# A two-block network with 64 routed experts on one core: another cut of the first expert blocks, token rows kept once in fp32, 18 weight buffers, another end

## The chip, the core and the metric

The kernel runs on one core of a Trainium2 chip, in one launch. The core has TensorE (PE, whose weight loads the profile lists as PEld), VectorE (DVE), ScalarE (ACT), GpSimd (POOL) and SyncE (SP), which here issues nearly all loads. The metric is the device time of one launch in microseconds; the profile has a span, from the first to the last instruction, and the time of its own execution, which is a little longer.

## What is computed

512 tokens of 1024 numbers pass an even and an odd attention layer, then a Fourier and state-space mixer, and at last 64 routed experts and a norm. All but the last two stay as they are, so only these are shown.

```python
hn = _rmsnorm(x, ffn_norm_g[i])
x = x + _hier_moe(hn, ...)          # and then _rmsnorm(x, final_norm_g)

def _hier_moe(h, wg, bg, we, be, w_gate, w_up, w_down):
    g_prob = softmax(ht @ wg + bg);  p_g, g_idx = top_k(g_prob, 1)      # one of 8 groups
    e_sel = (ht @ we + be) of that group                                # its 8 experts
    top_l, top_i = top_k(e_sel, 2)
    gate_w = p_g * softmax(top_l);  expert = g_idx * 8 + top_i
    ...
    def expert_block(args):                                             # per expert, on its tokens
        a = jax.nn.silu(xb @ w_gate[e]) * (xb @ w_up[e])
        return a @ w_down[e]
    ...
    y = y_pad[dest] * w_s[:, None]
    out = segment_sum(y, tok_s, num_segments=t)                         # two experts per token, added
```

All is fp32. An expert has three weights of 2 MB (`w_gate`, `w_up` 1024x512, `w_down` 512x1024), 384 MB in all, each read once.

## The kernel before

The residual stream is kept transposed as `h[k]`, eight tiles of 128 features by 512 tokens. `mix` ends with eight steps; behind each of them `feed3(k)` takes the new `h[k]`: its squares for the norm, its scaled copy for the router's matmul (`self.logits`, 72 rows), and its transposes into token rows, four 128x128 blocks on PE. The rows are written three times: unscaled into `x3`, the running sum of the residual and the experts; and times the norm's gain as a high and a low fp32r part `hn`.

`route` is a chain of small DVE operations with some matmuls: logits, best group, best two experts, the place of each token within its expert (`slot`), the rank of the experts by count, a table of tokens and weights per block (`tab`). The work is cut into blocks of 128 rows. The first four experts are fixed, so their blocks need no ranking; the others are sorted by count, and the fullest come next. The first eight (`WIDE`) experts stand two to a block with 64 rows each, the 56 others four to a block with 32 rows each: 18 blocks. What doesn't fit is done by `moe_rest`, a loop that runs as often as there are experts with more tokens than rows (no pass in the profiled execution: each of the three weights is issued x128, which is what the blocks need).

Per pair of blocks `slot_rows` makes 0/1 selection matrices on DVE, and `rows` gathers the tokens' rows transposed by matmuls with them (L1979, hi and lo part one after the other). Per block `hidden` does the gate and up matmuls (L1997), `turned` four transposes, `result` the down matmuls (L2020); `combine` adds the rows back into `x3` by matmuls (L1942, L1943) and DVE additions (L1944). The experts of a block stand side by side on PE, each on its own columns. `moe_pairs` orders this: it puts parts of the previous block's combine and the next pair's gather into the present block.

The weights come as tiles `ew` of 128x2048 fp32 (1 MB), two per weight, 384 in all, on SP's queue in the order of use (`moe_pieces`, `moe_prefetch`). A tile takes the next buffer of a rotation (`w_tile`): four opened while the mixer still runs (`m_e0`, `E_EARLY`) and eleven after it (`m_e`, `E_MORE`). A load waits on SP until the last matmul that reads its buffer is done, and all later loads wait behind it. The last two blocks are ordered apart: their gate and up tiles first, then the down tiles, the very last of them fetched by columns (`by_col`), so that the results can be finished half by half (`last_results`, L1955 to L1963) with the final norm right behind them (`final`, L2080 to L2094).

## Time and profile before

| | before |
|---|---|
| median of 3 runs | 2388.55 us (2381.56 to 2389.39) |
| profiled execution | 2389.68 us |
| its span | 2387.9 us |
| mean granted TensorE clock | 0.958 of full speed |
| busy in the span: PE, DVE, ACT, POOL | 89%, 47%, 28%, 18% |
| DMA over the span | 546.35 MB, mean 229 GB/s |

The strip of the page cuts the span into 40 equal slices and gives busy tenths for each engine, the granted clock, and GB/s. The chain that ended last is followed back from the last instruction. In timelines a row is one instruction or a few like it, with its start; the idle time before it and what ended that stand in brackets.

### The profile page before, as it was taken

The numbers are of one execution on the slowest core, as the hardware profiler recorded it, in microseconds if no ns is written. First come the engines' busy times: TensorE is split into PE (matmuls) and PEld (weight loads), VectorE is DVE, ScalarE is ACT, GpSimd is POOL, SyncE is SP. The second block draws the span as 40 slices with busy tenths as digits, with TensorE's granted clock in tenths as the row PEclk, the third lists the DMA queues.
The fourth block names the chain that finished last, engine by engine and source line by source line (L and its number), as shares of the span: only waits on it lengthen the run. The fifth ranks groups of instructions, "written<-read, shape, count | busy, mean of one in ns | idle before, by whom it ended". The sixth has DMA issues, their size and how long they took to land. (4 is left out here: it accounts for less than half of the span.)

```text
span 2387.9 us, 30369 instructions
## 1 busy us (share of the span) xinstructions
PE 2132.0 (89%) x11370; PEld 1398.3 (59%) x11370; DVE 1116.5 (47%) x2239; ACT 665.3 (28%) x1278; POOL 437.7 (18%) x473
## 2 busy tenths in 40 slices
PE   8989998999999999999999969988888888787865
PEld 7878886887788888889868744432222222222311
DVE  7687869674455665665744542421111111111102
ACT  6623223335445555543325410000000000000001
POOL 1235655300024333311311400000000000000000
PEclk9989999999999999989999979999999999999988
DMA  5213334554221212124352477999999999999996
GB/s 187 86 59 108 113 105 138 146 167 161 76 89 45 71 54 63 54 67 151 108 167 87 170 294 318 383 400 420 421 421 421 421 421 421 421 421 421 420 421 237
DMA packets 110832, 546.35 MB, mean 229 GB/s; under 512 B 13552, under 2 KB 14493, under 8 KB 62554
## 3 DMA queue, kind: packets, MB, share of 16 engines
q1 hardware_dynamic: 105834, 529.66, 58.0%
q0 software_dynamic: 4528, 13.67, 1.7%
q8 instruction: 91, 1.49, 0.3%
q10 hardware_dynamic: 320, 1.05, 0.1%
...
HBM read 531.22 MB, written 15.20 MB: 229 GB/s over the span
## 5 line engine op out<-in xcount | busy, mean ns | idle before, releaser
L1997 PE MATMUL mps<-ew,xt 128*32 128x512 f32 (+1 forms) x2048 | 391.1, 654 | 89.1 <-DMA ew<-in_w_up 48.8
L314 PE MATMUL ps<-uh,wh 128*128 128x512 f32 (+1 forms) x728 | 291.9, 401 | 7.7 <-ACT uh L309 7.3
L316 PE MATMUL ps<-uh,wl 128*128 128x512 f32 (+1 forms) x728 | 287.6, 395 | 3.5 <-DVE wl L345 3.5
L343 ACT ACTIVATE wh<-wraw 128x1024 fp32r<-128x1024 f32 (+5 forms) x187 | 186.8, 999 | 368.8 <-PE ps L315 268.7
L315 PE MATMUL ps<-ul,wh 128*128 128x512 f32 (+1 forms) x728 | 287.0, 394 | 0.5 <-DVE ul L310 0.5
L1997 PEld LDWEIGHTS mps<-ew,xt 128*32 128x32 f32 (+1 forms) x2048 | 93.2, 121 | 330.2 <-issue 164.3
L2020 PE MATMUL mps<-ew,s 128*32 128x512 f32 (+1 forms) x960 | 226.2, 620 | 38.5 <-DMA ew<-in_w_down 28.3
L345 DVE TENSOR_TENSOR wl<-wraw,wh 128x1024 fp32r<-128x1024 f32 (+4 forms) x172 | 218.4, 1270 | 49.1 <-ACT wh L343 47.2
L2082 POOL TENSOR_TENSOR ew<-x,ew 128x512 f32<-128x512 f32 x4 | 5.0, 1281 | 933.9 <-DVE x L1963 933.9
L2020 PEld LDWEIGHTS mps<-ew,s 128*32 128x32 f32 (+1 forms) x960 | 57.1, 115 | 195.4 <-issue 100.5
L314 PEld LDWEIGHTS ps<-uh,wh 128*128 128x128 f32 (+1 forms) x728 | 138.0, 190 | 39.9 <-ACT uh L309 7.3
L316 PEld LDWEIGHTS ps<-uh,wl 128*128 128x128 f32 (+1 forms) x728 | 137.6, 189 | 34.5 <-DVE wl L345 4.1
L315 PEld LDWEIGHTS ps<-ul,wh 128*128 128x128 f32 (+1 forms) x728 | 137.8, 189 | 28.4 <-DVE ul L310 1.0
L310 DVE SCALAR_TENSOR_TENSOR s<-mps,tab,s 128x512 fp32r<-128x512 f32 x36 | 27.0, 750 | 260.8 <-ACT s L309 260.0
L309 ACT ACTIVATE s<-mps,tab 128x512 fp32r<-128x512 f32 x36 | 24.8, 688 | 421.3 <-PE mps L2020 407.0
L2002 DVE SCALAR_TENSOR_TENSOR s<-mps,tab,s 128x512 f32<-128x512 f32 x18 | 13.5, 751 | 268.6 <-PE mps L1997 267.0
L314 PE MATMUL ps<-yh,wh 128*128 128x512 f32 x320 | 130.2, 409 | 1.9 <-DVE s L310 1.9
L316 PE MATMUL ps<-yh,wl 128*128 128x512 f32 x320 | 128.0, 400 | 1.7 <-DVE wl L345 1.7
L315 PE MATMUL ps<-yl,wh 128*128 128x512 f32 x320 | 128.9, 403 | 0.4 <-DVE yl L300 0.2
L1007 POOL TENSOR_SCALAR s<-s,n_sm 128x128 f32<-128x128 f32 (+3 forms) x96 | 110.1, 1165 | 8.4 <-DVE n_sm L998 4.9
L1944 DVE TENSOR_TENSOR x<-mps,x 128x512 f32<-128x512 f32 x128 | 83.6, 686 | 47.0 <-PE mps L1943 46.9
L2001 ACT ACTIVATE s<-mps,tab 128x512 f32<-128x512 f32 x18 | 12.4, 688 | 313.9 <-PE mps L1997 313.9
...
## 6 DMA issues: line engine op xcount, KB each, us to landing
ew<-in_w_gate SPq DMA_DIRECT2D x128, 1024.0 KB, 19.8
ew<-in_w_up SPq DMA_DIRECT2D x128, 1024.0 KB, 19.8
ew<-in_w_down SPq DMA_DIRECT2D x128, 1024.0 KB, 19.8
...
b<-in_od_w SPq DMA_DIRECT2D x32, 256.0 KB, 4.5
...
```

What stands on the lines that cost most here:

```text
L309: self.nc.scalar.activation(hi, src, AF.Copy, scale=col)
L310: self.nc.vector.scalar_tensor_tensor(lo, src, col, hi, ALU.mult, ALU.subtract)
L314: mm(out, l[0], r[0], start=start, stop=False)
L315: mm(out, l[0], r[1], start=False, stop=False)
L316: mm(out, l[1], r[0], start=False, stop=stop)
L343: nc.scalar.activation(hi, raw, AF.Copy)
L345: (nc.gpsimd if on_pool else nc.vector).tensor_tensor(lo, raw, hi, ALU.subtract)
L1007: nc.gpsimd.tensor_scalar(p[:, :w_], p[:, :w_], sm[:, br, hh:hh + 1], None, ALU.mult)
L1944: nc.vector.tensor_tensor(self.x3[:, b, cs], o, self.x3[:, b, cs], ALU.add)
L1997: nc.tensor.matmul(o[rs], xt[k][:, c0 + z * m:c0 + z * m + m], self.expert_rhs(w[i][z], k, 512, 0, 512), start=k == 0, stop=k == KD - 1)
L2002: nc.vector.scalar_tensor_tensor(act, h[1], r, act, ALU.mult, ALU.mult)
L2020: self.nc.tensor.matmul(y[hf][rs], at[:, k, rs], self.expert_rhs(w[-1][r], k, D, hf * 512, 512), start=k == 0, stop=k == 3)
```

## The change

`FIXED, WIDE` become 4, 4: block 0 has the four fixed experts with 32 rows each (24 tiles), blocks 1 and 2 have the four fullest ranked ones with 64 rows each (12 tiles), 14 blocks of four follow: 17 blocks. Block 0 has a gather of its own, 128 rows wide; blocks 1 and 2 share the next one, which now stands ahead of block 0's transposes. Eight weight buffers are opened early and ten later, 18 in all.

The rows are kept once, in fp32 and without the gain (`hn`). The gain is a 128x8 tile (`gperm`) and is applied when the gathered rows leave PSUM. The gather is one fp32 matmul where two fp32r ones were. `x3` is first written by block 0's combine. The transposes of `h[4]` to `h[7]` move from `feed3` into `route`, with their copies on ScalarE. At the end the previous block is combined before `last_results`, which then adds only its own rows, and the final norm takes one reciprocal root for all four token blocks. Small tiles move between pools.

```diff
-FIXED, WIDE = 4, 8
-BLOCKS = WIDE // 2 + (64 - WIDE) // 4
-GROUPS = BLOCKS // 2
+FIXED, WIDE = 4, 4
+BLOCKS = 1 + WIDE // 2 + (64 - FIXED - WIDE) // 4
+GROUPS = 1 + BLOCKS // 2
 SH_RET = 2
 NSA_FILL = 1, 2, 2, 2
-E_EARLY, E_MORE = 4, 11
+LATE = 4
+E_EARLY, E_MORE = 8, 10
...
-        self.hn = [self.t(self.mp, [P, NB, KD, P], "hn" + x, F32R) for x in "hl"]
+        self.hn = self.t(self.mp, [P, NB, KD, P], "hn")
...
-        tp = self.ps("tr")
-        self.transposes(tp, [(b * P, h[:, b * P:(b + 1) * P]) for b in range(NB)])
-        tv = tp.rearrange("p (b d) -> p b d", b=NB)
-
-        xg, g = self.s([P, NB, P]), self.gr[k // 4][:, k % 4 * P:k % 4 * P + P]
-        nc.vector.tensor_tensor(xg, tv, g.unsqueeze(1).to_broadcast([P, NB, P]), ALU.mult)
-        nc.vector.tensor_copy(self.x3[:, :, k * P:(k + 1) * P], tv)
-        hi, lo = (y[:, :, :, 16 * k:16 * k + 16] for y in self.hn)
-        xg = xg.rearrange("p b (m k) -> p b k m", k=KD)
-        nc.scalar.activation(hi, xg, AF.Copy)
-        nc.gpsimd.tensor_tensor(lo, xg, hi, ALU.subtract)
+        if k < LATE:
+            self.into_rows(k, nc.vector.tensor_copy)
         for j in range(max(0, k - 1), k if k < KD - 1 else KD):
             nc.tensor.matmul(self.logits[:72], self.wr[j // 4][:, j % 4], self.gx[j], start=j == 0, stop=j == KD - 1)
-        if k % 2 == 0 and len(self.early) < E_EARLY:
+        if len(self.early) < E_EARLY:
             self.moe_prefetch(len(self.early) + 1)
+
+    def into_rows(self, k, copy):
+
+        tp = self.ps("tr")
+        self.transposes(tp, [(b * P, self.h[k][:, b * P:(b + 1) * P]) for b in range(NB)])
+        copy(self.hn[:, :, :, 16 * k:16 * k + 16], tp.rearrange("p (b m k) -> p b k m", b=NB, k=KD))
...
-        self.gr = [self.load(self.bcast(a["ffn_g"], 512, c), [P, 512], y(x)) for c, x in ((0, "yh"), (512, "yl"))]
+        self.gperm = self.load(bass.AP(tensor=a["ffn_g"].tensor, offset=a["ffn_g"].offset, ap=[[KD, P], [1, KD]]), [P, KD],
+                               lambda sh: self.t(self.mp, sh, "gperm"))
...
+        for k in range(LATE, KD):
+            self.into_rows(k, nc.scalar.copy)
...
+        def further(out, pos):
+
+            v.tensor_scalar(out, pos, float(FIXED), 32.0, ALU.is_ge, ALU.mult)
+            v.scalar_tensor_tensor(out, pos, float(FIXED + WIDE), out, ALU.is_lt, ALU.mult)
+        further(more, cl[:, :64])
...
-        return 2 if p < WIDE // 2 else 4
+        return 2 if 1 <= p <= WIDE // 2 else 4
 
     def experts(self, p):
 
         n = self.parts(p)
-        e = 2 * p if n == 2 else WIDE + 4 * (p - WIDE // 2)
-        if e < FIXED:
-            return list(range(e, e + n))
+        if p == 0:
+            return list(range(n))
+        e = FIXED + 2 * (p - 1) if n == 2 else FIXED + WIDE + 4 * (p - 1 - WIDE // 2)
...
-        iota, sh = self.it[:, :256], [P, 2, 256]
+        n = 256 if j else P
+        iota, sh = self.it[:, :n], [P, 2, n]
         slot, j = (self.slot[1], j - 1) if j else (self.slot[0], 0)
         sel = []
         for b2 in range(2):
-            first, both = self.s(sh), self.s(sh, F32R)
+            first, both = self.s(sh), self.s(sh)
...
-                nc.vector.tensor_tensor(self.x3[:, b, cs], o, self.x3[:, b, cs], ALU.add)
-
-    def last_results(self, p, at, oht, w, old, out):
+                if p:
+                    nc.vector.tensor_tensor(self.x3[:, b, cs], o, self.x3[:, b, cs], ALU.add)
+                else:
+                    by_m = lambda x: x.rearrange("p (m k) -> p m k", k=KD)
+                    x = self.hn[:, b, :, hf * 64:hf * 64 + 64].rearrange("p k m -> p m k")
+                    nc.vector.tensor_tensor(by_m(self.x3[:, b, cs]), by_m(o), x, ALU.add)
+
+    def last_results(self, p, at, oht, w, out):
...
-                for i, (l, r) in enumerate([(old[2], x_) for x_ in old[1][hf]] + [(oht, x_) for x_ in yp]):
-                    nc.tensor.matmul(o, l[:, b * P:(b + 1) * P], r, start=i == 0, stop=i == 3)
+                for i in range(2):
+                    nc.tensor.matmul(o, oht[:, b * P:(b + 1) * P], yp[i], start=i == 0, stop=i == 1)
...
-                    for y in range(2):
-                        nc.tensor.matmul(tp[:, k * n:k * n + n], self.hn[y][:, b, k0 + k], one,
-                                         start=i == 0 and y == 0, stop=i == len(sel) - 1 and y == 1)
+                    nc.tensor.matmul(tp[:, k * n:k * n + n], self.hn[:, b, k0 + k], one, start=i == 0,
+                                     stop=i == len(sel) - 1)
             t_ = self.t(self.mp, [P, per, n], "xt", bufs=4)
-            (nc.scalar.copy if k0 // per % 2 else nc.vector.tensor_copy)(t_, tp.rearrange("p (k t) -> p k t", k=per))
+            for k in range(per):
+                g, o = self.gperm[:, k0 + k:k0 + k + 1], tp[:, k * n:k * n + n]
+                if k % 2:
+                    nc.scalar.activation(t_[:, k], o, AF.Copy, scale=g)
+                else:
+                    nc.vector.tensor_scalar(t_[:, k], o, g, None, ALU.mult)
...
-            act = self.hidden(xt, p % 2 * P, lambda: scales(p), w, n)
-            if p % 2:
+            act = self.hidden(xt, P if p and p % 2 == 0 else 0, lambda: scales(p), w, n)
+            if p % 2 == 0:
...
-        self.last_results(end + 1, *final, self.moe_weights(1, n), old, out)
+        self.combine(*old)
+        self.last_results(end + 1, *final, self.moe_weights(1, n), out)
...
-            elif b % 2:
-                r = ss[:, 0, b - 1:b + 1]
-                v.tensor_tensor(r, r, ss[:, 1, b - 1:b + 1], ALU.add)
+            elif b == NB - 1:
+                r = ss[:, 0]
+                v.tensor_tensor(r, r, ss[:, 1], ALU.add)
                 v.tensor_scalar(r, r, 1.0 / D, EPS, ALU.mult, ALU.add)
-                r = self.rsqrt(r, [P, 2])
-                for i in range(2):
-                    y, c = o[b // 2][:, i], r[:, i:i + 1]
+                r = self.rsqrt(r, [P, NB])
+                for i in range(NB):
+                    y, c = o[i // 2][:, i % 2], r[:, i:i + 1]
                     nc.scalar.activation(y[:, lo], y[:, lo], AF.Copy, scale=c)
-                    v.scalar_tensor_tensor(y[:, hi], self.x3[:, b - 1 + i, hi], c, self.fin_row[:, hi], ALU.mult,
-                                           ALU.mult)
+                    v.scalar_tensor_tensor(y[:, hi], self.x3[:, i, hi], c, self.fin_row[:, hi], ALU.mult, ALU.mult)
                     for k in range(2):
-                        (nc.sync, nc.scalar)[k].dma_start(ov[b - 1 + i, k], y[k * 64:k * 64 + 64])
+                        (nc.sync, nc.scalar)[k].dma_start(ov[i, k], y[k * 64:k * 64 + 64])
```

First, SP's queue where the mixer ends (`yh`, `yl` hold the router's weights and the gain; `ew` are expert tiles; what an issue waits for stands in brackets). Before:

```order
L320 DMA yl_12896<-in_wr 128x288 [waits PE_49]
L320 DMA yh_12894<-in_wr 128x288 [waits PE_49]
L1879 DMA ew_12834<-in_w_gate 128x2048 [waits Pool_49]
L320 DMA yh_12898<-in_ffn_g 128x512 [waits PE_49]
L320 DMA yl_12900<-in_ffn_g 128x512
L1879 DMA ew_12922<-in_w_gate 128x2048 [waits DVE_49]
L1879 DMA ew_12990<-in_w_gate 128x2048 [waits DMAHW7_49]
L1879 DMA ew_13058<-in_w_gate 128x2048 [waits DMAHW0_49]
L1879 DMA ew_13290<-in_w_up 128x2048 [waits DMAHW1_49,DVE_49]
L1879 DMA ew_13292<-in_w_up 128x2048 [waits DMAHW2_49]
L1879 DMA ew_13294<-in_w_up 128x2048 [waits DMAHW3_49,PE_49]
L1879 DMA ew_13296<-in_w_up 128x2048 [waits DMAHW4_49,DMAHW5_49,DVE_49,PE_49]
```

After:

```order
L321 DMA yl_12895<-in_wr 128x288 [waits PE_49]
L321 DMA yh_12893<-in_wr 128x288 [waits PE_49]
L1885 DMA ew_12834<-in_w_gate 128x2048 [waits Pool_49]
L1885 DMA ew_12913<-in_w_gate 128x2048
L1885 DMA ew_12941<-in_w_gate 128x2048
L1885 DMA ew_12975<-in_w_gate 128x2048
L1885 DMA ew_13003<-in_w_gate 128x2048 [waits DMAHW0_49,DVE_49]
L1885 DMA ew_13031<-in_w_gate 128x2048 [waits DMAHW1_49]
L1885 DMA ew_13053<-in_w_gate 128x2048 [waits DMAHW2_49]
L1885 DMA ew_13081<-in_w_gate 128x2048 [waits DMAHW3_49]
L1885 DMA ew_13261<-in_w_up 128x2048 [waits DMAHW4_49,DVE_49]
L1885 DMA ew_13263<-in_w_up 128x2048 [waits DMAHW5_49,PE_49]
```

All eight gate tiles of block 0 now stand behind the router's two loads, the two gain loads are gone, and what the first eight issues wait for is less.

Second, PE at the end of `hidden` of block 0: L1774 and L1778 rank the experts (L1773 and L1777 after), L1815 is the table's matmul (L1821 after), L472 the transposes of block 0's hidden rows (L473 after), L2020 its result (L2036 after). Before, L1997 behind the table is already block 1's `hidden`:

```order
L1997 MATMUL mps_13391<-ew_13296,xt_13385 64x512
L1774 MATMUL mps_13436<-s_13434,ones_85 128x64
L1778 MATMUL mps_13436<-s_13439,mc_12904 1x64
L1815 MATMUL mps_13476<-s_13465,s_13469 128x54 [waits DVE_49,Pool_49]
L1815 MATMUL mps_13476<-s_13465,s_13469 128x54 x3
L1815 MATMUL mps_13476<-s_13465,s_13474 128x54 [waits DVE_49,Pool_49]
L1815 MATMUL mps_13476<-s_13465,s_13474 128x54 x3
L1838 MATMUL mps_13516<-fl_13512,mc_12904 64x1
L1997 MATMUL mps_13571<-ew_13555,xt_13316 64x512 [waits DMAHW1_49,Activation_49]
L472 MATMUL mps_13492<-ident_81,s_13408 128x128 [waits DVE_49]
L472 MATMUL mps_13492<-ident_81,s_13408 128x128 x3
L1997 MATMUL mps_13571<-ew_13557,xt_13316 64x512 [waits DMAHW2_49]
```

After, with L2013 for `hidden` and L1990 for the gather:

```order
L2013 MATMUL mps_13354<-ew_13275,xt_13333 32x512
L1821 MATMUL mps_13458<-s_13447,s_13451 128x51 [waits DVE_49,Pool_49]
L1821 MATMUL mps_13458<-s_13447,s_13451 128x51 x3
L1821 MATMUL mps_13458<-s_13447,s_13456 128x51 [waits DVE_49,Pool_49]
L1821 MATMUL mps_13458<-s_13447,s_13456 128x51 x3
L1844 MATMUL mps_13565<-fl_13560,mc_12901 64x1
L1990 MATMUL mps_13484<-s_13475,hn_12837 128x256 [waits DVE_49] x2
...
L1990 MATMUL mps_13520<-s_13480,hn_12837 128x256 x2
L473 MATMUL mps_13532<-ident_81,s_13387 128x128 [waits Activation_49]
L473 MATMUL mps_13532<-ident_81,s_13387 128x128 x3
L2036 MATMUL mps_13578<-ew_13539,s_13537 32x512 [waits DMAHW4_49,DVE_49]
```

The ranking matmuls moved ahead of the last 13 matmuls of `hidden`, and the gather for blocks 1 and 2 (32 matmuls of 256 columns, two to most rows) now stands between the table and block 0's transposes and result.

Third, PE in the last block, between its first and second half of the result (L1955, L1967 after); `xt` and `s` on the right hold rows of this block and, before, of the previous one:

```order
L1955 MATMUL mps_17563<-ew_17498,xt_17426 32x512 [waits DMAHW1_49,DVE_49]
L1962 MATMUL mps_17531<-s_17527,xt_17428 128x512 [waits Activation_49]
L1962 MATMUL mps_17539<-s_17527,xt_17428 128x512
L1962 MATMUL mps_17531<-s_17528,xt_17428 128x512 [waits DVE_49]
L1962 MATMUL mps_17539<-s_17528,xt_17428 128x512
L1962 MATMUL mps_17547<-s_17482,s_17446 128x512 [waits DVE_49]
L1962 MATMUL mps_17547<-s_17483,s_17446 128x512
L1962 MATMUL mps_17547<-s_17527,xt_17428 128x512
L1962 MATMUL mps_17547<-s_17528,xt_17428 128x512
L1962 MATMUL mps_17555<-s_17482,s_17446 128x512 [waits DVE_49]
L1962 MATMUL mps_17555<-s_17483,s_17446 128x512
L1962 MATMUL mps_17555<-s_17527,xt_17428 128x512
```

After:

```order
L1967 MATMUL mps_17242<-ew_17185,xt_17081 32x512 [waits DMAHW0_49,PE_49]
L1974 MATMUL mps_17218<-s_17214,xt_17083 128x512 [waits DVE_49,Activation_49]
L1974 MATMUL mps_17224<-s_17214,xt_17083 128x512 [waits DVE_49]
L1974 MATMUL mps_17218<-s_17215,xt_17083 128x512 [waits DVE_49]
L1974 MATMUL mps_17224<-s_17215,xt_17083 128x512
L1974 MATMUL mps_17230<-s_17214,xt_17083 128x512 [waits DVE_49]
L1974 MATMUL mps_17230<-s_17215,xt_17083 128x512
L1974 MATMUL mps_17236<-s_17214,xt_17083 128x512 [waits DVE_49]
L1974 MATMUL mps_17236<-s_17215,xt_17083 128x512
L1967 MATMUL mps_17242<-ew_17187,xt_17081 32x512 [waits DMAHW1_49]
L1967 MATMUL mps_17242<-ew_17189,xt_17081 32x512 [waits DMAHW2_49]
L1967 MATMUL mps_17242<-ew_17191,xt_17081 32x512 [waits DMAHW3_49]
```

Two additions per output where four were, and the second half's matmuls stand directly behind them.

## Rows read from the trace of the kernel before

**Rows 1.** Page part 2, bytes moved in 40 equal slices of the span.
```profile
GB/s 187 86 59 108 113 105 138 146 167 161 76 89 45 71 54 63 54 67 151 108 167 87 170 294 318 383 400 420 421 421 421 421 421 421 421 421 421 420 421 237
```

**Rows 2.** Windows: us, busy time (instructions) by engine, clock, DMA share, GB/s.
```profile
1339.10:1439.10 100.00, 76.65 (x363) 48.92 (x363) 48.16 (x133) 27.37 (x35) 23.62 (x20) 0.83 0.64 250
1439.10:1562.50 123.40, 119.23 (x604) 52.66 (x604) 40.38 (x65) 10.60 (x16) 0.00 (x0) 1.00 0.90 364
1562.50:2332.00 769.50, 622.72 (x3120) 201.40 (x3113) 133.04 (x218) 33.46 (x51) 0.00 (x0) 0.95 1.01 421
2332.00:2360.30 28.30, 22.06 (x101) 6.62 (x94) 3.98 (x6) 3.40 (x7) 1.59 (x2) 1.00 0.97 363
2360.30:2387.90 27.60, 9.71 (x48) 3.75 (x47) 10.43 (x39) 7.58 (x17) 3.42 (x3) 0.76 0.30 82
```

**Rows 3.** Page part 6, DMA issues: count, KB each, median us to landing.
```profile
ew<-in_w_gate SPq DMA_DIRECT2D x128, 1024.0 KB, 19.8
```

**Rows 4.** Timeline of SP's queue: start us, us, what is issued, count.
```profile
1339.12 0.43 SPq L1879 DMA_DIRECT2D ew<-in_w_gate  x1
...
1351.77 0.80 SPq L1879 DMA_DIRECT2D ew<-in_w_up  x2
...
1439.11 0.33 SPq L1879 DMA_DIRECT2D ew<-in_w_down  x1
```

**Rows 5.** Timeline of PE, block 0: start, us, count [idle before, releaser].
```profile
1390.41 0.58 PE L1979 MATMUL mps<-s,hnh 128*128 128x256 f32 x1 [1.49 <-DVE s L1924]
...
1415.86 0.43 PE L1774 MATMUL mps<-s,ones 64*128 64x64 f32 x2
...
1423.65 3.67 PE L1815 MATMUL mps<-s,s 128*128 128x54 f32 x16 [7.16 <-POOL s L1809]
...
1429.68 1.97 PE L1997 MATMUL mps<-ew,xt 128*64 128x512 f32 x2 [2.06 <-ACT s L2001]
...
1434.41 1.70 PE L2020 MATMUL mps<-ew,s 128*64 128x512 f32 x2
```

**Rows 6.** Windows of 5 us, columns as in group 2.
```profile
1430.00:1435.00 5.00, 5.00 (x11) 1.49 (x10) 1.71 (x4) 0.00 (x0) 0.00 (x0) 0.50 0.00 0
1435.00:1440.00 5.00, 5.00 (x24) 1.54 (x24) 0.21 (x1) 0.00 (x0) 0.00 (x0) 0.92 0.00 0
1440.00:1445.00 5.00, 5.00 (x26) 1.80 (x24) 1.58 (x3) 1.38 (x2) 0.00 (x0) 1.00 0.94 324
```

**Rows 7.** Chain that ended last: start us, us on the chain, what, count.
```profile
1355.37 0.86 PE ps L1648 x2
1356.22 0.58 PE ps L472 x4
...
1463.84 6.98 PE mps L1979 x56
...
1472.30 6.87 PE mps L2020 x31
1479.17 13.73 PE mps L1997 x62
1492.90 0.43 PE mps L1942
1493.34 0.24 PE mps L1943
...
1555.45 7.01 PE mps L1997 x64
```

**Rows 8.** Timeline of DVE, first selection and the last scalings.
```profile
1389.14 0.69 DVE L1920 TENSOR_TENSOR s<-mc,slot 128x512 f32<-128x512 f32 x1
...
2377.30 1.41 DVE L2091 SCALAR_TENSOR_TENSOR ew<-x,rs_y,ew 128x512 f32<-128x512 f32 x2
```

**Rows 9.** Timeline of PE, the last block's second half.
```profile
2362.78 3.63 PE L1955 MATMUL mps<-ew,xt 128*32 128x512 f32 x28
```

**Rows 10.** Window behind the last landing, columns as in group 2.
```profile
2360.00:2364.00 4.00, 4.00 (x22) 1.49 (x24) 1.24 (x2) 1.45 (x4) 3.72 (x3) 1.00 0.08 30
```

More of the change, by code (lines that the diff above doesn't have):

```diff
@@ L889, in odd @@
         ys = self.mem_branch(w, u, kv, 2)
-        gates = self.t(self.cp, [P, NB, 36], "gates")
+        gates = self.t(self.gb, [P, NB, 36], "gates")
         m31 = self.load(a["m31"], [P, 1], lambda s: self.small(s, "m31", bufs=1))
@@ L970, in nsa_scores @@
         pr = {}
-        oc, ec = self.ps(), self.small([P, 3, 32], "n_pe", bufs=2)
+        oc, ec = self.ps(), self.t(self.gb, [P, 3, 32], "n_pe", bufs=2)
         nc.gpsimd.memset(ec[:, :, ncmp:], 0.0)
@@ L1002, in nsa_scores @@
                 if br == 0:
-                    pr[br, hh] = self.small([P, 3, 32], "n_pc", bufs=6)
+                    pr[br, hh] = self.t(self.gb, [P, 3, 32], "n_pc", bufs=6)
                     nc.gpsimd.tensor_scalar(pr[br, hh], p.unsqueeze(1).to_broadcast([P, 3, 32]), sm[:, br, hh:hh + 1],
@@ L1155, in ssm_params @@
         self.d_kt = dr([P, NG, P], "ssm_kt")
-        self.rho = self.t(self.cp, [P, NG], "ssm_rho")
+        self.rho = self.t(self.up, [P, NG], "ssm_rho")
         pool = self.right("ssm")
@@ L1732, in route @@
         v.scalar_tensor_tensor(place, row(zg, list(s2)), 8.0, ze, ALU.mult, ALU.add)
-        v.tensor_scalar(place, place, 64.0, 9 * 4096.0, ALU.mult, ALU.add)
+        v.tensor_scalar(place, place, 32.0, 9 * 2048.0, ALU.mult, ALU.add)
         v.tensor_tensor(ge, lgg, last(gm, s8), ALU.subtract)
@@ L1781, in route @@
         more = self.t(mp, [P, 64], "r_more")
-        v.tensor_scalar(more, cl[:, :64], float(WIDE), 32.0, ALU.is_lt, ALU.mult)
+        def further(out, pos):
+            v.tensor_scalar(out, pos, float(FIXED), 32.0, ALU.is_ge, ALU.mult)
+            v.scalar_tensor_tensor(out, pos, float(FIXED + WIDE), out, ALU.is_lt, ALU.mult)
+        further(more, cl[:, :64])
         v.tensor_tensor(q, o12, row(cl[:, :64], s64), ALU.mult)
@@ L1786, in route @@
         v.tensor_reduce(pt, q, AX.X, ALU.add)
-        v.tensor_scalar(mt, pt, float(WIDE), 32.0, ALU.is_lt, ALU.mult)
+        further(mt, pt)
         v.tensor_tensor(mt, xf, mt, ALU.subtract)
         v.tensor_scalar(ff, mt, 32.0, 100000.0, ALU.is_ge, ALU.mult)
-        v.tensor_scalar(mt, pt, 32.0, 32.0 * WIDE, ALU.mult, ALU.add)
-        v.scalar_tensor_tensor(mt, pt, 64.0, mt, ALU.mult, ALU.min)
+        v.tensor_scalar(mt, pt, 32.0, -32.0 * FIXED, ALU.mult, ALU.add)
+        v.tensor_scalar(mt, mt, 0.0, 32.0 * WIDE, ALU.max, ALU.min)
+        v.scalar_tensor_tensor(mt, pt, 32.0, mt, ALU.mult, ALU.add)
         v.tensor_tensor(mt, mt, xf, ALU.add)
@@ L1795, in route @@
         sj, sq = [P, 2 * NB, GROUPS - 1], [P, 2 * NB, BLOCKS]
-        v.scalar_tensor_tensor(self.slot[1], row(self.it[:, 1:GROUPS], sj), -256.0, last(mt, sj), ALU.mult, ALU.add)
+        v.scalar_tensor_tensor(self.slot[1], row(self.it[:, 1:2 * GROUPS - 2:2], sj), -128.0, last(mt, sj), ALU.mult,
+                               ALU.add)
         d, inb = new(sq), new(sq)
@@ L1833, in route @@
         fl = self.t(mp, [64, 1], "fl")
-        v.tensor_scalar(fl, pos, float(WIDE), 32.0, ALU.is_lt, ALU.mult)
+        further(fl, pos)
         v.tensor_tensor(fl, cnt, fl, ALU.subtract)
@@ L1926, in slot_rows @@
                 sel.append((b, both[:, z]))
-        return Later(self.rows(sel, 256))
+        return Later(self.rows(sel, n))
     def places(self, p, new=None):
@@ L2111, in moe_rest @@
             for b in range(NB):
-                xt = Later(self.rows([(b, self.identr)], P))
+                xt = Later(self.rows([(b, self.ident)], P))
                 y = self.result(self.turned(self.hidden(xt, 0, lambda: self.rtok[:, b:b + 1], ws, 1)), ws, 1)
```

12 lines of the change are left out of this document (5 added, 7 removed).

## The prediction

> **What bounds the kernel now.** I first read the page's strip of 40 slices [rows 1]: for the first 23 slices the moved bytes swing between 45 and 187 GB/s, then they climb over four (294 to 400), and from the 28th, about 1612 us, they stand at 420 or 421 until the last. That is the experts' weights. Then the stretches of the expert part [rows 2]: 421 GB/s over 769.5 us is the plateau, so a 1 MB tile (1.0486 MB) takes 1.0486 / 0.421 = 2.49 us, and the 384 tiles that page part 6 counts (three weights, x128 each [rows 3]) take 956 us however they are ordered. So the time is: when the stream starts, plus 956, plus every microsecond in which it stands still, plus what comes after its last byte.
>
> It starts with SP's first `ew` at 1339.12 and not continuously [rows 4]: four gate tiles, two up tiles at 1351.77, and so on behind slots that open late; the 15 buffers are then full and wait for experts. The first tile that waits for block 0's result (the 24th, a down tile) goes out at 1439.11. So in the 100 us to 1439.1 only 23 tiles have come in (250 GB/s x 100 us = 25.0 MB, less 0.8 MB of router and gain loads) where about 40 would fit. From there to 1562.5 it runs at 364 GB/s instead of 421: 123.4 x (1 - 364/421) = 16.7 us stood still. PE is 119.2 of those 123.4 us busy: blocks of two cost PE more than their tiles cost the stream. Later it loses 28.3 x (1 - 363/421) = 3.9 us at the end (tiles fetched by columns), and 27.6 us pass after the last landing [rows 2].
>
> Why 1439? PE's timeline [rows 5] is one chain: the gather for blocks 0 and 1 starts at 1390.41, `hidden(0)` ends at 1415.86, two small matmuls rank the experts, DVE and GpSimd make the table's operands, the table's matmuls (L1815) start 7.16 us idle later, at 1423.65, and the result of block 0 starts at 1434.41, in part at half clock (0.50 at 1430 to 1435, 0.92 right behind it [rows 6]).
>
> **The change part by part.**
>
> *Buffers and the opening.* 18 buffers for 15, and eight early ones: SP's order now has eight gate tiles right behind the router's loads. Block 0 is now a block of four experts with 24 tiles; 18 are loaded early and the 16 of gate and up come free by the end of `hidden(0)`. So 34 tiles can be in when block 0's first down tiles come free, where 23 were: 11 x 2.49 = **-27.4 us**, if time allows. It does: gate tiles come free from about 1400, and 16 x 2.49 = 40 us from there end at about 1440.
>
> *When block 0's first down tiles come free.* The transposes of the last four mixer steps leave the mixer (0.58 us for a step's four on the chain [rows 7]: 4 x 0.58 = 2.3 us); they go behind the router's first transposes, where PE waits for DVE anyway. If ACT's copies there were late they would cost at most the same 2.3. The selection is 128 wide for 256, some 0.6 us less (its first operation took 0.69 [rows 8], the two behind it about as much). So the gather starts at about 1390.4 - 2.9 = 1387.5. It and `hidden(0)` took 1415.9 - 1390.4 = 25.5 us; now 32 fp32 matmuls of 128 columns stand for 64 of 256 in fp32r. The trace has no such form; the nearest rows are the router's fp32 matmul, 512 columns in two records of 0.86 us together, and `hidden` of a block of two: 62 records in 13.73 us, two experts side by side, two records each, so 13.73 x 4/62 = 0.88 for 512 columns [rows 7]. By columns that is 0.43 for 256 and 0.215 for 128. So 32 x 0.215 = 6.9 against 64 x 0.12 = 7.7 (56 in 6.98 [rows 7]), and `hidden` of a block of four costs 14.0 (64 of its 128 records in 7.01 us), that of two 13.9 [rows 7]. `hidden(0)` ends at about 1412.3. Since the order puts the ranking matmuls 13 matmuls before that end, they run at about 1409.4 (13 x 0.22 earlier). From them to the table 7.8 us passed; I add 0.5 for two or three more of the tiny DVE operations between: table at 1417.7, done 3.7 later, at 1421.4.
>
> Now comes what speaks against the change. Before, the result of block 0 followed the table after one scaling and four transposes. Now the whole gather for blocks 1 and 2 stands between: selection on DVE (two pairs, with 0.69 for the first operation of each; some 4 us with the table's copy), PE from about 1425.5; 32 fp32 matmuls of 256 columns, 30 of them behind the last operand, at 0.43 = 12.9 us. The first ones run at half clock: before, the clock rose some 5 us after PE got dense work at 1429.68 [rows 5, 6], so I add 2 us. That is 1440.4; transposes and copy 1.5; the result's first half 7.1/2 = 3.5 (31 records in 6.87 [rows 7]): **1445.4** for 1439.1, **+6.3 us**. Bounds: 0.12 a matmul if fp32 cost what fp32r does (1436, but the 16 freed tiles are hardly in before 1441, so nothing is won below that); all at half clock, +12 or so. I take 0.43, since both rows are fp32 themselves.
>
> [...]
>
> *Two blocks of two instead of four.* The stream stood still 16.7 us because PE needed 13.9 (hidden) + 7.1 (result) [rows 7] and 5.4 for combine (8 x (0.43 + 0.24) [rows 7]) per two-expert block, 26 us of PE for 12 tiles (29.9 us of stream), plus gathers, table and transposes. A block of four needs the same 26 for 59.8 us of stream. From 1445.4 PE now has 3.5 left of result 0, two blocks of 26, and one fp32 gather, 32 x 0.43 = 13.8: about 71 us, to 1517. In 71 us the stream brings 28 tiles, 62 in all; what is freed by the end of `hidden(2)` (44) plus 18 allows 62. So it waits little: some 4 us for the down tiles of block 2, some 4 for the gates of block 3, and 2 us from issue to first byte (324 GB/s in 1440 to 1445 [rows 6] after the issue at 1439.11: the stream ran from about 1441.1): 10 for 16.7, **-6.7**. Bounds: 3 (only the issue) and 16.7 (as before).
>
> *Rows kept once.* `x3` is no longer written in the mixer, hi/lo copies on ACT, DVE and GpSimd go; these engines wait for PE there, so nothing. The norm gain moves to the copies out of PSUM, per column group: two operations where one copy was, alternating engines, under a PE that takes 8 x 0.43 us per tile. Nothing; if the copies were the limit, 1 us a gather. Adding `hn` in block 0's combine reads in permuted order, 8 DVE operations under `hidden(1)`.
>
> *The end.* Old results are combined before, so two matmuls per output for four; results of the second half start sooner behind their tiles (the last 28 records start at 2362.78 [rows 9], 2.5 us after the last landing: 30 GB/s in the 4 us from 2360 on are 0.12 MB, so it is at 2360.3 [rows 10]). Then the last add and one rsqrt chain for four instead of two one behind the other (the second pair's scaling starts at 2377.30, behind both chains [rows 8]): three quarters of the second half's 3.63 us run before the last landing, 2.7, and by estimate 0.75 of matmuls between the adds and 0.5 of rsqrt go: **-4.0** (bounds -1 and -5).
>
> **Sum**: -27.4 + 6.3 - 6.7 - 4.0 = -31.8 us. The span of 2387.9 becomes 2356.1; the profiled execution's own time is 1.8 above its span, 2389.68 - 31.8 = 2357.9, and it is 1.1 above the median, so **2357 us** as a median.
>
> **Rivals.**
> 1. *The clock stays at half* through the gather and the first results. For it: 0.50 up to 1435 [rows 6], behind gaps like those that now stand before the gather. Against: it was 0.92 after 5 us of dense work. 32 matmuls at 0.86 and the result: +12 to +15, 2369 to 2372. 0.09.
> 2. *Two blocks of two are still PE-bound as before*, fp32 gathers eating what the smaller number of blocks gives; idle stays 16.7 and the second gather's 13.8 - 7.7 = 6.1 us come on top: 2357 + 6.7 + 6.1 = 2370. For it: PE 97% busy in that stretch. Against: half as many of these blocks. 0.13.
> 3. *Better*: gather at the fp32r price or hidden under selection, 1441, idle 3, end 22.6: 2357 - 4.4 - 7 - 1 = about 2345. 0.09.
> 4. *Slower: a fixed expert overflows.* Its rows fall from 64 to 32. One token too many (33) makes the clean-up loop run: six tiles (14.9 us) and four token blocks, each 16 hidden and 8 result matmuls of fp32 with 0.86 or so per 512 columns (20.6 us, 83 in all): +98, about 2455. The reference's routing gives the first four experts 19, 5, 27 and 20 tokens, and only three others have over 31, which are among the four wide ones. 0.02.
> 5. *The stream does not use the buffers* (18 opened, but the 16 freed tiles wait for the table or a register): 27.4 falls to some 10 (only the three buffers and the smaller first wait), 2374. 0.07.
>
> The forecast itself has 0.60, and its own range is 2349 to 2364. A range that leaves out rival 4, half of 5 and the ends of 3: **2343 to 2374**. 0.3% (7 us) is what a measurement of this kernel tells from no change. Faster by more than that needs under 2381: all but rival 4 and the edge of 5, 0.95; same 0.02; slower 0.03.
>
> **What would show it.** 18 `ew` issues without a wait on block 0 and all of them in by about 1396; the first issue that waits for block 0's result, the 35th, near 1445; fp32 gather matmuls at 0.43 pitch with PEclk up after the first few; 415 to 421 GB/s instead of 364 in the 120 us behind; last landing near 2332; 23 to 24 us behind it. Wrong if the stream has holes of over 5 us after 1445, or if the clean-up loop issues any tile.

## The result, and the profile after

The changed kernel takes 2359.41 us (median of 4 runs, 2357.57 to 2362.91), 0.9879 of the kernel before (95% interval 0.9863 to 0.9894): 29 us less. The forecast was 2357 with 2343 to 2374 as its range. The forecast holds, but its four terms together were 9 us too good, one of them alone by that much, and two effects that stood in no term, +9 and -13 us, brought 4 us of it back. The profiled execution of the change took 2362.91 us with a span of 2361.1, 26.8 less than the span before.

Page parts 2 (the line of moved bytes) and 6 of the changed kernel, which answer to [rows 1] and [rows 3]:

```profile
GB/s 183 94 59 108 116 100 138 141 167 152 72 102 64 38 73 72 43 59 137 90 163 108 152 333 381 339 392 426 427 427 426 427 426 427 427 427 427 427 426 252
...
ew<-in_w_gate SPq DMA_DIRECT2D x128, 1024.0 KB, 19.5
ew<-in_w_up SPq DMA_DIRECT2D x128, 1024.0 KB, 19.5
ew<-in_w_down SPq DMA_DIRECT2D x128, 1024.0 KB, 19.5
```

The plateau is 427 GB/s, not 421, and a tile lands 19.5 us behind its issue, not 19.8. So 384 tiles take 384 x 1.0486 / 0.427 = 943 us, 13.4 less than the 956 of before. Each weight is still issued x128: the clean-up loop makes no pass.

Windows of the changed kernel (us, busy time and instructions by engine, clock, DMA share, GB/s): from the first expert tile to the 35th, to 1562.5, the plateau, the end of the stream, and what is behind it, as in [rows 2]:

```profile
1348.40:1451.60 103.20, 89.33 (x499) 62.47 (x501) 42.66 (x137) 22.21 (x37) 10.92 (x12) 0.87 0.86 349
1451.60:1562.50 110.90, 104.55 (x502) 42.26 (x498) 33.36 (x49) 8.07 (x13) 0.00 (x0) 0.98 0.88 355
1562.50:2305.00 742.50, 613.65 (x3061) 213.64 (x3052) 133.92 (x227) 37.76 (x63) 0.00 (x0) 0.96 1.01 427
2305.00:2336.50 31.50, 27.15 (x118) 7.88 (x114) 10.05 (x16) 4.14 (x10) 2.22 (x2) 1.00 0.93 364
2336.50:2361.10 24.60, 6.42 (x36) 2.08 (x34) 8.24 (x23) 6.73 (x15) 2.79 (x3) 0.68 0.27 88
```

SP's queue, which answers to [rows 4], with the first expert tile and the 35th, the first that waits for block 0's result:

```profile
1348.43 0.91 SPq L1885 DMA_DIRECT2D ew<-in_w_gate  x2
...
1451.59 0.33 SPq L1885 DMA_DIRECT2D ew<-in_w_down  x1
```

PE in block 0, which answers to [rows 5] (start us, us, count, idle before and what ended it):

```profile
1394.61 7.68 PE L1990 MATMUL mps<-s,hn 128*128 128x128 f32 x44 [1.03 <-DVE s L1931]
1402.21 3.64 PE L2013 MATMUL mps<-ew,xt 128*32 128x512 f32 x32
...
1416.59 0.43 PE L1773 MATMUL mps<-s,ones 64*128 64x64 f32 x2
...
1425.00 3.66 PE L1821 MATMUL mps<-s,s 128*128 128x51 f32 x16 [4.23 <-POOL s L1815]
1428.58 0.37 PE L1844 MATMUL mps<-fl,mc 64*64 64x1 f32 x2
1430.47 15.81 PE L1990 MATMUL mps<-s,hn 128*128 128x256 f32 x64 [1.52 <-DVE s L1931]
1446.12 0.63 PE L473 MATMUL mps<-ident,s 128*128 128x128 f32 x4
1447.54 1.04 PE L2036 MATMUL mps<-ew,s 128*32 128x512 f32 x2 [0.78 <-DVE s L2026]
```

Where the stream ends, two windows of 1 us each of the kernel before, and two of the changed kernel (columns as above):

```profile
2361.00:2362.00 1.00, 1.00 (x4) 0.30 (x3) 0.48 (x1) 0.79 (x3) 1.00 (x2) 1.00 0.10 39
2362.00:2363.00 1.00, 1.00 (x8) 0.53 (x10) 0.00 (x0) 0.30 (x2) 1.00 (x2) 1.00 0.01 4
```
```profile
2335.00:2336.00 1.00, 1.00 (x6) 0.24 (x5) 1.00 (x2) 0.76 (x3) 1.00 (x2) 1.00 0.17 66
2336.00:2337.00 1.00, 1.00 (x12) 0.20 (x12) 0.26 (x1) 1.00 (x4) 1.00 (x2) 1.00 0.01 2
```

The last bytes land at about 2362.1 before (I had put 2360.3; but bytes still come in at 39 GB/s from 2361 to 2362 and at 4 in the next us) and 2336.1 after. With that the two spans divide as follows; the third line is what remains between the others:

| us | before | after | difference |
|---|---|---|---|
| first expert tile issued | 1339.1 | 1348.4 | +9.3 |
| 384 tiles at the plateau's rate | 956.4 | 943.0 | -13.4 |
| stream stands still, first issue to last landing | 66.6 | 44.7 | -21.9 |
| behind the last landing | 25.8 | 25.0 | -0.8 |
| span | 2387.9 | 2361.1 | -26.8 |

The first three terms of the forecast's sum (-27.4 + 6.3 - 6.7 = -27.8) are the third line here, -21.9. Worked out by itself it splits into three parts that make -21.8: 34 tiles for 23 are in at the first wait for block 0's result, 11 x 2.46 = -27.0; that wait comes 103.2 us behind the first issue instead of 100.0, +3.2; and behind it, up to 1562.5, the stream loses 110.9 x (1 - 355/427) = 18.7 us for 16.7, +2.0.

### The profile page after: what moved, and what is told of

It reads as the page before. It is cut to its first block, busy times and chain, and to the rows that moved or that the text cites. A ratio compares the mean times of both kernels' runs of the same rounds, so it can differ in the third digit from the quotient of the medians.

```text
span 2361.1 us, 30316 instructions
## 1 busy us (share of the span) xinstructions
PE 2131.4 (90%) x11350; PEld 1408.9 (60%) x11350; DVE 1109.2 (47%) x2229; ACT 661.2 (28%) x1289; POOL 422.7 (18%) x465
## 5 line engine op out<-in xcount | busy, mean ns | idle before, releaser
L2013 PE MATMUL mps<-ew,xt 128*32 128x512 f32 (+1 forms) x2048 | 383.4, 645 | 85.1 <-DMA ew<-in_w_up 47.9
L2013 PEld LDWEIGHTS mps<-ew,xt 128*32 128x32 f32 (+1 forms) x2048 | 86.5, 118 | 326.3 <-issue 170.7
L2036 PE MATMUL mps<-ew,s 128*32 128x512 f32 (+1 forms) x960 | 173.9, 608 | 25.7 <-DMA ew<-in_w_down 13.9
L1990 PE MATMUL mps<-s,hn 128*128 128x256 f32 (+1 forms) x576 | 135.0, 386 | 2.6 <-DVE s L1931 2.6
L1990 PEld LDWEIGHTS mps<-s,hn 128*128 128x128 f32 x576 | 104.4, 198 | 53.3 <-issue 33.5
L2036 PEld LDWEIGHTS mps<-ew,s 128*32 128x32 f32 (+1 forms) x960 | 49.0, 113 | 137.6 <-issue 79.7
L1998 DVE TENSOR_SCALAR xt<-mps,gperm 128x256 f32<-128x256 f32 (+1 forms) x36 | 16.8, 468 | 237.2 <-PE mps L2013 198.3
L311 DVE SCALAR_TENSOR_TENSOR s<-mps,tab,s 128x512 fp32r<-128x512 f32 x34 | 25.5, 751 | 188.4 <-ACT s L310 187.6
## 6 DMA issues: line engine op xcount, KB each, us to landing
ew<-in_w_gate SPq DMA_DIRECT2D x128, 1024.0 KB, 19.5
ew<-in_w_up SPq DMA_DIRECT2D x128, 1024.0 KB, 19.5
ew<-in_w_down SPq DMA_DIRECT2D x128, 1024.0 KB, 19.5
```

The source lines that it names most:

```text
L311: self.nc.vector.scalar_tensor_tensor(lo, src, col, hi, ALU.mult, ALU.subtract)
L1990: nc.tensor.matmul(tp[:, k * n:k * n + n], self.hn[:, b, k0 + k], one, start=i == 0, stop=i == len(sel) - 1)
L1998: nc.vector.tensor_scalar(t_[:, k], o, g, None, ALU.mult)
L2013: nc.tensor.matmul(o[rs], xt[k][:, c0 + z * m:c0 + z * m + m], self.expert_rhs(w[i][z], k, 512, 0, 512), start=k == 0, stop=k == KD - 1)
L2036: self.nc.tensor.matmul(y[hf][rs], at[:, k, rs], self.expert_rhs(w[-1][r], k, D, hf * 512, 512), start=k == 0, stop=k == 3)
```

## The experiments

All times are compared through the kernel before, run beside each of them. The two theories at the start: the total is right because the terms are; or it is right by chance, with a rate and a start that come from elsewhere.

**Both kernels once more.** No edit.

> The kernel before once more, unchanged. Theory (chance between executions): the mixer part in front of the experts runs longer or shorter by where half-clock stretches fall, so the first expert tile goes out anywhere within some 10 us of 1339, and the plateau's rate of 421 GB/s also moves by 1 to 2% between executions. Rival (the change does it): the first tile goes out at 1339 within 2 us and the plateau is 421 again.

> The changed kernel once more, unchanged. Theory (chance): the first expert tile goes out up to 10 us away from 1348.4, and the plateau may differ from 427 GB/s. Rival (the change does it): 1348 within 2 us and 427 again; then the moved small tiles cost 9 us and the 18 buffers give the stream 1.4%.

2385.37 and 2359.79 us. The rate is no chance: 421 and 427 GB/s again, from 1562.5 to 2300 us. The first tile went out at 1334.3 and 1346.2, 5 and 2 us earlier than the first time, so the start does scatter between executions. Over all profiles the four with the old layout of the small tiles start at 1334.3 to 1340.4, the ten with the new one at 1342.5 to 1352.1: the start is later by some 9 us on average, beyond that scatter.

**Where the buffers start in SBUF.** In the built programs the 15 buffers of before start 160 (eleven) and 32 bytes (four) past a multiple of 256 within a partition; the 18 of after start at multiples of 256. That is a by-product of which pools hold the small tiles. Two unused tiles move them:

```diff
+            pad = self.t(self.pool(st, "pad1"), [P, 24], "pad1", bufs=1)
+            self.nc.gpsimd.memset(pad, 0.0)
             self.eps += [(self.pool(st, "m_e"), E_MORE)] * E_MORE
...
+        pad = self.t(self.pool(self.rs, "pad0", side="right"), [P, 8], "pad0", bufs=1)
+        self.nc.gpsimd.memset(pad, 0.0)
         self.eps = [(self.pool(self.rs, "m_e0", side="right"), E_EARLY)] * E_EARLY
```

The widths are 24 and 8 here, 8 and 8 in the second kernel, and 40 and 24 in the third, which is the changed kernel.

> The kernel before with two small unused tiles that move its 15 weight buffers: eleven start at byte 25,760 + n x 8,192 of a partition (160 past a multiple of 256) and four at 32 past one; here all start at a multiple of 256. Theory (where a buffer starts sets the rate of its fill): the plateau goes from 421 to 427 GB/s and the time falls by about 380 x 0.035 = 13 us, to about 2376. Rival (the rate comes with the other parts of the change): 421 and within 4 us of the kernel before.

> The kernel before with smaller tiles in front: eleven buffers start 192 past a multiple of 256 (a multiple of 64) and four at a multiple of 256. If a start at a multiple of 64 is enough: 427 GB/s and 13 us less, as with starts at multiples of 256. If it takes a multiple of 256: 419 to 422 GB/s and within 5 us of the kernel before. [...]

> The changed kernel with two small unused tiles that put all its 18 buffers 160 bytes past a multiple of 256, where they start at multiples of 256. Theory (the start of a buffer sets the rate): 419 to 421 GB/s, 10 to 15 us more, about 2372. Rival (the rate comes with the other parts of the change): 427 and within 4 us of 2359.

2374.18 us (0.9938, 0.9915 to 0.9961), 2382.99 (0.9977, 0.9963 to 0.9990) and 2369.32 (0.9923, 0.9899 to 0.9947). The plateau of the three, one window each:

```profile
1562.50:2300.00 737.50, 603.62 (x3046) 197.22 (x3038) 131.21 (x215) 33.43 (x51) 0.00 (x0) 0.95 1.01 427
```
```profile
1562.50:2300.00 737.50, 600.87 (x3002) 193.59 (x3002) 130.39 (x214) 33.46 (x51) 0.00 (x0) 0.96 1.01 423
```
```profile
1562.50:2300.00 737.50, 610.51 (x2974) 210.26 (x2972) 132.16 (x224) 37.79 (x63) 0.00 (x0) 0.95 1.01 421
```

The start of the buffers sets the rate, in both kernels and both directions: the kernel before goes from 421 to 427 GB/s and gains 15 us by it alone (9 to 20 by the interval), the changed one goes from 427 to 421 and loses 10. Starts at 192 past a multiple of 256, a multiple of 64, are not enough: with eleven of fifteen there the rate is 423, a little above the 419 to 422 that was expected for that case. In all other versions of the changed kernel below the buffers start at multiples of 256.

**The number of buffers.** Edit: `E_EARLY, E_MORE = 8, 7`.

> The changed kernel with 15 weight buffers (eight early, seven later). Theory: three tiles fewer are in when block 0's down tiles come free, so the stream stands still 3 x 2.46 = 7.4 us longer: about 2367. Rival (the later holes are PE's and swallow it): within 2 us of 2359.

2366.56 us (0.9911, 0.9897 to 0.9925) for 0.9879: 7.6 us more, where 7.4 were expected; the two intervals leave some 5 us either way. In its trace the first tile that waits for block 0's result is the 32nd for the 35th, at 1445.6, 102.7 us behind the first issue.

**The early opening.** Edit: `E_EARLY, E_MORE = 4, 14`.

> The changed kernel with its 18 buffers split as 4 early and 14 later. Theory: the early opening matters only so far as the tiles are late for block 0; 18 tiles take 44 us and more than 60 pass between the first issue and the gather, so 0 to 5 us more: 2359 to 2364. Rival (eight early ones are what fills the buffers): fewer than 18 tiles are in when block 0 begins, and each missing one costs 2.46 us: over 2369.

2365.47 us (0.9900, 0.9885 to 0.9915): 5 us more by the ratios, at the edge of what the first theory allows. SP's queue and PE in its trace show where they come from:

```profile
1416.81 26.60 SPq L1885 DMA_DIRECT2D ew<-in_w_up  x4
```
```profile
1439.69 3.62 PE L2013 MATMUL mps<-ew,xt 128*32 128x512 f32 x26
1443.24 7.61 PE L1990 MATMUL mps<-s,hn 128*128 128x256 f32 x34
```

In this version the last matmuls of `hidden(0)` stand in the middle of the next gather on PE, not ahead of the table. So the up tiles that reuse their buffers wait: only 30 tiles are out before 1442.5, and the 35th goes out 108.6 us behind the first issue (1456.1 - 1347.5) for 103.2. In this trace it is the order on PE that costs; that fewer early tiles cost by themselves isn't shown.

**The blocks of before in the changed kernel.** The edit puts `FIXED, WIDE = 4, 8`, `BLOCKS`, `parts`, `experts`, the places in `route` and the position of the gathers back to the lines of before; 18 buffers, fp32 rows and the new end stay.

> The changed kernel with the blocks of before: four blocks of two (64 rows, the first two of them fixed), then 14 of four, and the gathers where they stood before. Theory (a block of four in front lets 34 tiles in before the first down tiles come free): with a block of two only 18 + 8 = 26 are in, 8 x 2.46 = 20 us; against that the result of block 0 no longer waits for a gather, some 10 us: about 2369, with holes as in the kernel before. Rival (it is the number and start of the buffers, not the blocks): within 4 us of 2359.

2384.24 us (0.9987, 0.9973 to 1.0001): 26 us more than the changed kernel, and more than either theory gave. PE at its start shows what was left out of that sum (columns as above):

```profile
1388.98 7.75 PE L1983 MATMUL mps<-s,hn 128*128 128x256 f32 x24 [1.43 <-DVE s L1924]
...
1403.19 3.72 PE L1983 MATMUL mps<-s,hn 128*128 128x256 f32 x16
...
1420.88 0.43 PE L1773 MATMUL mps<-s,ones 64*128 64x64 f32 x2
```

The first gather is 256 columns wide again, now in fp32: its matmuls take 17.2 us for 10.2, in front of everything, and the ranking comes 31.9 us behind the gather's start (1420.88 - 1388.98) where the changed kernel needs 22.0 (1416.59 - 1394.61). So the first wait for block 0's result ends 100.3 us behind the first issue, hardly sooner than the 103.2 of the changed kernel, with 26 tiles in for 34. And behind it four blocks of two with fp32 gathers hold the stream longer:

```profile
1442.80:1562.50 119.70, 116.83 (x514) 57.06 (x514) 38.57 (x61) 11.34 (x19) 0.00 (x0) 1.00 0.80 330
```

That is 119.7 x (1 - 330/427) = 27.2 us lost for 18.7. The new blocks (block 0 of four with its narrow gather, two blocks of two for four) carry the change: without them buffers, rate, fp32 rows and end together are worth 3 us. The edit puts all of the blocks back at once, so it does not part block 0 from the others.

**The gather behind the result.** In `moe_pairs` the gather of even blocks moves behind their result:

```diff
-            if p % 2 == 0:
-                xt = self.slot_rows(p // 2 + 1).all()
-            elif old:
+            if p % 2 and old:
                 old = self.combine(*old)
...
                 self.scaled_split(*ys[hf], y[hf], self.gw[:, p:p + 1])
+            if p % 2 == 0:
+                xt = self.slot_rows(p // 2 + 1).all()
```

> The changed kernel with the gathers of blocks 0, 2, 4, ... behind the block's result instead of ahead of its transposes. Theory (the gather in front holds back the down tiles, so the stream stands still): block 0's first down tiles come free about 15 us earlier, the holes of 6 us before them and of 9 us in block 2 shrink, and the time falls by 5 to 15 us, to 2345 to 2354. Rival (PE sets the pace in the blocks of two): PE does the same work, the holes only move one block on, and the time stays within 3 us of 2359.

2358.28 us (0.9863, 0.9848 to 0.9877) for 0.9879; the intervals overlap. The rival holds. The changed kernel's stream has two holes behind the first wait:

```profile
1445.00:1455.00 10.00, 9.22 (x75) 3.71 (x77) 1.98 (x5) 0.47 (x1) 0.00 (x0) 1.00 0.45 159
1510.00:1550.00 40.00, 38.64 (x190) 18.79 (x190) 10.41 (x17) 3.27 (x6) 0.00 (x0) 1.00 0.66 248
```

With the gather behind the result the first goes (424 GB/s), but one as large (5.7 us for 6.3) opens at 1465 to 1475, and the long one (17.5 for 16.8) stands at 1530 to 1550:

```profile
1445.00:1450.00 5.00, 3.74 (x10) 2.58 (x11) 4.96 (x8) 0.01 (x1) 0.00 (x0) 0.79 1.00 424
...
1465.00:1475.00 10.00, 10.00 (x48) 4.64 (x48) 0.48 (x1) 1.02 (x3) 0.00 (x0) 1.00 0.49 182
...
1535.00:1540.00 5.00, 5.00 (x25) 4.41 (x24) 0.97 (x2) 0.95 (x2) 0.00 (x0) 1.00 0.00 0
1540.00:1545.00 5.00, 5.00 (x27) 4.10 (x29) 0.58 (x2) 0.47 (x1) 0.00 (x0) 1.00 0.00 0
```

In these rows of the holes PE is busy 9.2 of 10 us, 38.6 of 40, 10.0 of 10 and 10.0 of 10: by them it is the amount of its work there, not the order within it.

**The blocks of two later.** Ranks 4 to 7 (the fullest) change place with the eight behind them, so blocks 1 and 2 have four experts each, and 3 and 4 two:

```diff
+FIXED, WIDE, FIRST = 4, 4, 2
+W0 = FIXED + 4 * FIRST
...
+        v.tensor_scalar(by, pos, float(FIXED), 4.0 * FIRST, ALU.is_ge, ALU.mult)
+        v.tensor_scalar(step, pos, float(FIXED + WIDE), -4.0 * FIRST - WIDE, ALU.is_ge, ALU.mult)
+        v.tensor_tensor(by, by, step, ALU.add)
+        v.tensor_scalar(step, pos, float(W0 + WIDE), float(WIDE), ALU.is_ge, ALU.mult)
+        v.tensor_tensor(by, by, step, ALU.add)
+        v.tensor_tensor(pos, pos, by, ALU.add)
...
-        return 2 if 1 <= p <= WIDE // 2 else 4
+        return 2 if FIRST < p <= FIRST + WIDE // 2 else 4
```

`further`, the places and `experts` use `W0` where the wide blocks begin, and a third unused tile, 48 columns wide, stands ahead of the early buffers, so that all still start at multiples of 256.

> The changed kernel with the two blocks of two fullest experts as blocks 3 and 4 instead of 1 and 2; six more tiny DVE operations in the ranking. Theory (the stream's holes of some 17 us between 1510 and 1550 come from PE's work in two blocks of two straight behind block 0, with only 18 tiles of lead): behind two blocks of four the buffers are full and hide it, the holes shrink to under 5 us, and the time falls by 10 to 15 us, to about 2347. Rival (the holes come from the gathers in fp32 and the buffers' number, whatever the order): the holes move two blocks on and the time stays within 4 us of 2359.

2341.66 us (0.9810, 0.9788 to 0.9833), 16 to 18 us below the changed kernel, more than the 10 to 15 expected, and some 46 below the one before. The stretch from 1430 to 1562.5 ran at 352 GB/s in the changed kernel and now runs at 406, which is 132.5 x (406 - 352)/427 = 16.8 us; the hole of 1510 to 1550 is gone (426 GB/s), the one in front of block 0's down tiles is left:

```profile
1430.00:1562.50 132.50, 124.90 (x600) 57.47 (x604) 39.66 (x63) 10.92 (x19) 0.00 (x0) 0.97 0.86 352
```
```profile
1430.00:1562.50 132.50, 120.74 (x665) 51.37 (x665) 34.64 (x54) 9.28 (x16) 0.00 (x0) 0.99 0.97 406
```

**Both of the last two.**

> The changed kernel with the two blocks of two as blocks 3 and 4 and the gathers of even blocks behind the block's result. Theory: the one hole left, some 6 us between 1440 and 1450, lies in front of block 0's down tiles; with the gather behind the result they come free 15 us earlier, the hole goes, and the blocks of four behind it have time for the gather: 4 to 7 us less than with the wide blocks moved alone, about 2336. Rival (the hole only moves, as it did when the gather was moved alone): 2341.

2341.99 us (0.9807, 0.9793 to 0.9820): the rival again. The hole at 1440 to 1450 is gone and stands at 1460 to 1470 (194 GB/s), and another of 3.5 us opens at 1645 to 1655 (278). The version with the blocks moved alone is as fast, and the simpler one.

**The end of before in the changed kernel.** `last_results`, `final` and the call are the lines of before.

> The changed kernel with the end of before (four matmuls per output, two reciprocal roots). Theory, from the trace of the changed kernel (27.6 us behind the last landing, as before): the new end gains nothing, and the time stays within 2 us of 2359. Rival (the prediction's term): 4 us more, 2363.

2364.10 us (0.9894, 0.9879 to 0.9909): by the ratios 3.6 us more, near the rival, with intervals that overlap. In its profile the last bytes land at 2336.1 (of a span of 2363.4), so 27.3 us pass behind them, and 25.0 with the new end; the 27.6 that the expectation took for the changed kernel is not in its trace. The new end is worth about 2 us by the profiles and up to 4 by the times.

## Why the prediction was right, and where it was not

**Buffers and the opening, -27.4.** Held: 34 tiles are in at the first wait, -27.0. Three buffers alone are 7.6 us, the new blocks 26.

**Block 0's first down tiles, +6.3.** The chain is as described, only a little shorter: +3.2. Counted from the first expert tile, the table began 76.6 us behind it (1425.00 - 1348.43); I had put 1417.7 - 1339.1 = 78.6. From the gather's start to the ranking 22.0 us passed for the 21.9 of the sum, although block 0's own gather took 10.2 for 6.9, partly at half clock (granted 0.51 from 1390 to 1400). That the sum held there is luck in part: the 25.5 us of before, to which it added only differences, held half-clock time too (0.76 from 1390 to 1400). The gather for blocks 1 and 2 starts 1.8 us behind the table's last matmul (4.1 forecast). Its selection on DVE begins only behind the table, as forecast:

```profile
1429.14 0.68 DVE L1927 TENSOR_TENSOR s<-mc,slot 128x512 f32<-128x512 f32 x1
```

But the first matmuls need only the first pair of selections, and start at 1430.47 while DVE makes the second. The gather takes 15.65 us for the 14.9 of the sum: 32 matmuls at 0.49 on average, the first of them at half clock. At full clock, from 1435 to 1446, they go at 0.42: the price of 0.43 by columns held. Rival 1 did not come: the clock is 0.50 from 1430 to 1434, where the gather starts, and 1.00 from 1435 on.

**Two blocks of two instead of four, -6.7: the step that failed.** The stream loses 18.7 us behind the first wait, not 10, and its holes there, 6 and 17 us, are the sign of being wrong that the forecast named (over 5 us after 1445). I had PE done with both blocks 71 us behind 1445.4; it took from 1451.6 to 1536.8. The groups of that stretch (line, form, count, busy us, mean ns, idle before):

```profile
L2013 PE MATMUL mps<-ew,xt 128*64 128x512 f32 x128 | 35.4, 600 | 0.0
L2036 PE MATMUL mps<-ew,s 128*64 128x512 f32 x64 | 15.9, 655 | 1.6 <-DVE s L2026 1.6
L1990 PE MATMUL mps<-s,hn 128*128 128x256 f32 x64 | 14.9, 386 | 0.0
L1949 PE MATMUL mps<-s,s 128*128 128x512 f32 x16 | 7.5, 466 | 1.2 <-DVE x L1956 0.9 <-DVE x L1952 0.3
L1950 PE MATMUL mps<-s,s 128*128 128x512 f32 x16 | 6.7, 421 | 0.4 <-DVE s L311 0.3
L2036 PE MATMUL mps<-ew,s 128*32 128x512 f32 x38 | 4.5, 592 | 0.0
```

Two `hidden` are 35.4 us where I had 27.8, two results 15.9 for 14.2, the gather 14.9 for 13.8. The combines' 14.2 (L1949 and L1950) count records that overlap; from the start of one matmul to that of the next they take 10.7, the 10.8 of the sum. `hidden` was priced from a run of its own, and here it alternates with the other matmuls:

```profile
1465.22 0.40 PE L1950 MATMUL mps<-s,s 128*128 128x512 f32 x1
1465.55 1.07 PE L2013 MATMUL mps<-ew,xt 128*64 128x512 f32 x2
1466.55 0.50 PE L1949 MATMUL mps<-s,s 128*128 128x512 f32 x1
...
1481.54 8.83 PE L2036 MATMUL mps<-ew,s 128*64 128x512 f32 x32 [0.78 <-DVE s L2026]
...
1529.72 7.09 PE L2036 MATMUL mps<-ew,s 128*64 128x512 f32 x32 [0.78 <-DVE s L2026]
```

Two records between two combines hold PE for 1.00 us, where two of a run took 0.44. Of the two results the second took the 7.1 of the sum, the first 8.8, with the clock granted at 0.83 from 1480 to 1490. The transposes (1.4) and 4 us of waits stood in no price. With PE waiting some 4 us in 85, rival 2 (PE-bound as before) is what happened, and it was given 0.13. That the position of these blocks matters and not the fp32 gather's place in them is what the two moves show: 16 to 18 us less for the one, nothing clear for the other.

**Rows kept once, 0.** Not nothing in one place: block 0's additions with the permuted read take 1041 ns where the plain ones take 688, and PE waited 0.9 us for them (the L1949 group above):

```profile
L1956 DVE TENSOR_TENSOR x<-mps,hn 128x512 f32<-128x512 f32 x8 | 8.1, 1041 | 11.1 <-PE mps L1950 11.1
...
L1952 DVE TENSOR_TENSOR x<-mps,x 128x512 f32<-128x512 f32 x8 | 5.3, 688 | 5.7 <-PE mps L1950 5.7
```

Small, as the text had it.

**The end, -4.0.** -0.8 between the two profiles, some -2 against the old end in the changed kernel. The 2.7 us of matmuls that were to run ahead of the last landing rested on a landing put 1.8 us too early: before, the last 28 records started 0.6 us behind it (2362.78 - 2362.2), not 2.5. In the changed kernel the combine of the block before stands in front of the first half's matmuls, and the second half's end 4.0 us behind the landing, hardly sooner than the 4.2 of before; the additions behind them take 4.9 for 5.7, and the one chain of roots with its four scalings 6.5 where two chains with theirs took 6.6.

**In no term.** The rate, -13.4, and the start, +9.3. The forecast took both from the profile of before as if the change could not touch them; but the diff moves small tiles between pools, and so it moves the address of everything behind them. Of the span's 26.8 us the rate and the start give 4.1, so what the four terms speak of gave 22.7, where they summed to 31.8: without the two the kernel would stand at about 2389.7 - 22.7 = 2367 by its profiled execution, still in the range but 9 us above the 2357.9 forecast for it, and nearer to rival 2's 2370. That the median came within 3 us of the forecast is partly luck: 4.1 us by the two, and 2.4 because the profiled execution (2362.91) lies 3.5 above the median, where 1.1 was forecast. Part of the later start is the clock. The windows from 415 to 440 us of the kernel before and of the changed one:

```profile
415.00:440.00 25.00, 22.43 (x119) 17.99 (x120) 19.47 (x42) 8.92 (x15) 8.47 (x15) 0.93 0.52 147
```
```profile
415.00:440.00 25.00, 23.48 (x102) 18.39 (x103) 14.71 (x33) 7.09 (x12) 4.75 (x9) 0.73 0.32 87
```

From 400 to 450 the clock is 0.97 in all four profiles with the old layout; with the new one it is 0.86 in four of ten, 0.93 in three and 0.97 in three, and SP falls 4 to 6 us behind there in the four at 0.86. But the three at 0.97 also start late, at 1342.5 to 1344.1: about 6 us of the 9 are not that stretch of clock. They gather in small steps between 450 us and the first expert tile. Which of the moved tiles does it was not tried; it stays open.
